# Two-layer MoE network on one core: expert choice by index among all 32 experts, counts issued later, two chunks gathered ahead, two-column Newton steps as tensor-scalar

## The chip, the cores and the metric

One NeuronCore of one Trainium2 chip runs the whole program in one launch. The metric is the device time of a run in microseconds (us); the kernel before takes 2264.09 us, the median of three runs.

## The reference

Two blocks of two layers follow each other on 256 tokens of width 1024, all in f32. The change lies in the first block, whose layers are an attention (layer 0) or a retention (layer 1) followed by a hierarchical mixture of experts. What that mixture computes:

```
p_group = softmax(xf @ wr_g + br_g);  pg, gi = top_k(p_group, 1)          # 4 groups
e_logits = (xf @ wr_e + br_e).reshape(T, 4, 8)
e_in = sum over groups of e_logits * one_hot(gi)                          # the 8 of the chosen group
pv, pi = top_k(softmax(e_in), 2)
gates = pg * pv / sum(pv);  expert_id = gi * 8 + pi
y = sum over both experts of gates * ((silu(a) * b) @ w_down[e]),  a, b = split(xf @ w_gu[e])
```

An expert's `w_gu` is 1024 x 1024 and its `w_down` 512 x 1024; there are 32 experts in each layer. The second block (gated recurrence, convolution, feed-forward) takes the first one's output; its context half does not depend on it and is woven into the mixtures as side work.

## The kernel before, in words

The program is written for Tile: each engine's instructions keep an order that a scheduler makes of the program's order and of priorities (`high_priority`), with semaphores for every dependence. All large weight loads are issued by SP on one queue, in order, each into one of a ring of 1 MB buffers (`wt`, `wload`, `wload2`); a load is issued when the last reader of its buffer is done.

A mixture (`moe`, from line 881) holds all 32 experts as 8 passes of 4 experts, each with 32 slots. It goes like this.

1. Ahead of it lie loads for the first steps: pairs k = 0 and 1 of pass 0, and four half tiles for k = 2 (lines 887 to 904), then further pairs into the ring as far as it reaches.
2. The router: `route_half` finishes the logits on TensorE (lines 857 and 861), `logits` (line 868) makes the root mean square of two token columns by `rsqrt` (line 223), and `choose` (line 762) finds group and experts on VectorE. There `top` is MAX8 and FIND_INDEX8 over the 4 group logits (padded to 8); line 781 masks the 32 expert logits by the group, line 782 sums them to 8; `top` again, over 8; lines 786 and 788 set a mask of 8 and `spread` (line 796) widens it to the 32-wide mask `M`.
3. Ranks: matmuls of `M` with triangles (lines 914 to 916), `rk` (line 919), and the one-hot places `oh` (line 926) of the first four experts, at high priority; those of the other 28 experts are called later, at k = 4, at normal priority.
4. The gather for pass 0: TensorE multiplies tokens by places, in eight chunks of 128 features (line 941), each copied out of PSUM into `xg` by ScalarE or VectorE in turn (lines 176 and 178). Three chunks are issued, then the counts of every expert (two matmuls, lines 952 and 953, and three VectorE instructions, lines 955 to 958), and then the gate/up products of pass 0.
5. Those run over k = 0 to 7 (line 999): 8 matmuls each, which the trace shows as 16, four experts side by side on column tiles of 32. For pass 0 each k from 1 on first issues the next chunk, so that at step k chunk k + 2 stands ahead of it, until there are no more. At k = 4 come the other places, the gates (`gates_of`), the overflow gates and the scatter matrix of pass 0.
6. Then silu, a product, four transposes and the down products (line 1019). Passes 1 to 7 follow, with the gather of each in the middle of the pass before. The counts are read as register values only in pass 7 (`overflow`), to see whether any expert has more than 32 tokens.

`rsqrt` starts from a bit trick and makes three Newton steps. One column takes two tensor-scalar instructions for a step (lines 241 and 242), more columns take three tensor-tensor instructions (lines 244 to 246). Two columns occur in `logits`, in `raw` (start of attention and of retention, line 364) and in `centred` (line 1229, in the second block's mixers).

Of the kernel before, what the change touches and what calls it, by code (L numbers as in the profile page):

```python
# [8 lines left out]
F32 = mybir.dt.float32  # L9
# [10 lines left out]
NEG = -1e30  # L20
# [10 lines left out]

C_ID, C_LE, C_LT, C_GE, C_ONE = 0, 128, 256, 384, 512
C_Z, C_LOW, C_UP = 640, 768, 896
C_IOTA, C_GRP, C_I8 = 1024, 1056, 1088
C_SEL, C_OFF = 1096, 1112
C_COS, C_SIN, C_RET = 1116, 1372, 1628
NCST = C_RET + 4 * 384


# [4 lines left out]
def constants():  # L44

    c = np.zeros((P, NCST), np.float64)
    r, q = np.arange(P)[:, None], np.arange(P)[None, :]
    c[:, C_ID:C_ID + P] = r == q
    c[:, C_LE:C_LE + P] = r <= q
    c[:, C_LT:C_LT + P] = r < q  # L50
    c[:, C_GE:C_GE + P] = r >= q
    c[:, C_ONE:C_ONE + P] = 1.0
    low, up = np.where(q <= r, 0.0, NEG), np.where(q >= r, 0.0, NEG)
    c[:, C_LOW:C_LOW + P] = low
    c[:, C_UP:C_UP + P] = up
    c[:, C_IOTA:C_IOTA + 32] = np.arange(1, 33)
    c[:, C_GRP:C_GRP + 32] = np.arange(32) // 8
    c[:, C_I8:C_I8 + 8] = np.arange(8)
# [34 lines left out]
class Net:  # L93
# [129 lines left out]
    def rsqrt(self, h, scaled=False):  # L223

        v, shape, n = self.nc.vector, list(h.shape), h.free_size()
        t = lambda k, d=F32: self.sm.tile(shape, d, tag="rs%s%d" % (k, n), name="rs")
        y, q = t("y", I32), t("q")
        v.tensor_scalar(y, h.bitcast(I32), -0.5, float(0x5f3759df), op0=ALU.mult, op1=ALU.add)
        y = y.bitcast(F32)
        if not scaled:  # L230
            g = t("g")
            v.tensor_scalar(g, h, -0.5, None, op0=ALU.mult)
        c = 1.0
        for _ in range(3):
            if scaled:
                v.tensor_scalar(q, y, h, y, op0=ALU.mult, op1=ALU.mult)
                v.tensor_scalar(y, q, -3.0 * c * c, y, op0=ALU.add, op1=ALU.mult)
                c = -2.0 * c ** 3
                continue
            if n == 1:  # L240
                v.tensor_scalar(q, y, g, y, op0=ALU.mult, op1=ALU.mult)
                v.tensor_scalar(y, q, 1.5, y, op0=ALU.add, op1=ALU.mult)
                continue
            v.tensor_tensor(q, y, y, op=ALU.mult)
            v.tensor_tensor(q, q, g, op=ALU.mult)
            v.scalar_tensor_tensor(y, q, 1.5, y, op0=ALU.add, op1=ALU.mult)
        assert not scaled or c == RS
        return y
# [513 lines left out]
    def choose(self, mp, L):  # L762


        nc, v = self.nc, self.nc.vector
        t = lambda n, *s, d=F32: mp.tile([P, 2] + list(s), d, name=n)
        grp = self.cst[:, C_GRP:C_GRP + 32]
        i8 = self.cst[:, C_I8:C_I8 + 8]

        def top(src, n):  # L770
            val, idx, f = t(n + "v", 8), t(n + "i", 8, d=U32), t(n + "f", 8)
            for b in range(2):
                v.max(out=val[:, b, :], in_=src[:, b, :])
            for b in range(2):
                v.max_index(out=idx[:, b, :], in_max=val[:, b, :], in_values=src[:, b, :])
            v.tensor_copy(f, idx)
            return val, f
        gv, gi = top(L[:, :, 0:8], "tg")
        sel, ein = t("sel", 32), t("ein", 8)
        for b in range(2):  # L780
            v.scalar_tensor_tensor(sel[:, b, :], grp, gi[:, b, 0:1], L[:, b, 8:40], op0=ALU.is_equal, op1=ALU.mult)
        v.tensor_reduce(ein, sel.rearrange("p b (g i) -> p b i g", g=4), axis=AX.X, op=ALU.add)
        ev, ei = top(ein, "te")
        m8, M = t("m8", 8), t("M", 32)
        for b in range(2):
            v.tensor_scalar(m8[:, b, :], i8, ei[:, b, 0:1], None, op0=ALU.is_equal)
        for b in range(2):
            v.scalar_tensor_tensor(m8[:, b, :], i8, ei[:, b, 1:2], m8[:, b, :], op0=ALU.is_equal, op1=ALU.add)
        self.spread(M, gi, m8)
        return M, gv, gi, ev, ei  # L790

    def spread(self, out, gi, w8):

        grp = self.cst[:, C_GRP:C_GRP + 32].rearrange("p (g i) -> p g i", g=4)
        for b in range(2):
            self.nc.vector.scalar_tensor_tensor(out[:, b, :].rearrange("p (g i) -> p g i", g=4), grp, gi[:, b, 0:1],
                                                w8[:, b:b + 1, :].to_broadcast([P, 4, 8]), op0=ALU.is_equal, op1=ALU.mult)

    def gates_of(self, mp, gv, gi, ev, ei):

        nc, v = self.nc, self.nc.vector
        t = lambda n, *s: mp.tile([P, 2] + list(s), F32, name=n)

        def softmax(val, n, name):
            neg, s = t(name + "n"), t(name + "s")
            p = t(name + "p", n)
            v.tensor_scalar(neg, val[:, :, 0], -1.0, None, op0=ALU.mult)
            for b in range(2):
                nc.scalar.activation(p[:, b, :], val[:, b, 0:n], AF.Exp, bias=neg[:, b:b + 1], accum_out=s[:, b:b + 1])
            v.reciprocal(s, s)  # L810
            v.tensor_tensor(p, p, s.rearrange("p (b o) -> p b o", o=1).to_broadcast([P, 2, n]), op=ALU.mult)
            return p
        pg, pe = softmax(gv, 4, "pg"), softmax(ev, 8, "pe")
        r, g2 = t("gr"), t("g2", 2)
        v.tensor_tensor(r, pe[:, :, 0], pe[:, :, 1], op=ALU.add)
        v.reciprocal(r, r)
        v.tensor_tensor(r, r, pg[:, :, 0], op=ALU.mult)
        v.tensor_tensor(g2, pe[:, :, 0:2], r.rearrange("p (b o) -> p b o", o=1).to_broadcast([P, 2, 2]), op=ALU.mult)
        a, c, G = t("ga", 8), t("gb", 8), t("G", 32)
        i8 = self.cst[:, C_I8:C_I8 + 8]  # L820
        for k, o in ((0, a), (1, c)):
            for b in range(2):
                v.tensor_scalar(o[:, b, :], i8, ei[:, b, k:k + 1], g2[:, b, k:k + 1], op0=ALU.is_equal, op1=ALU.mult)
        v.tensor_tensor(a, a, c, op=ALU.add)
        self.spread(G, gi, a)
        return G

    def route(self, l):
# [52 lines left out]
    def moe(self, l):  # L881
        nc, I, x, v = self.nc, self.I, self.x, self.nc.vector
        w_gu, w_down = I["expert_w_gu"][l], I["expert_w_down"][l]
        with ExitStack() as es:
# [61 lines left out]
                return xg, go()  # L946
            places(0, 4)
            xg, steps = gather(0, 1)
            for _ in range(3):
                next(steps, None)  # L950
            ps = self.g()
            nc.tensor.matmul(ps[:, 0:32], self.ones, M[:, 0, :], start=True, stop=False)
            nc.tensor.matmul(ps[:, 0:32], self.ones, M[:, 1, :], start=False, stop=True)
            cnt = mp.tile([P, 33], F32, name="cnt")
            v.tensor_copy(cnt[:, 0:32], ps[:, 0:32])
            v.tensor_reduce(cnt[:, 32:33], cnt[:, 0:32], axis=AX.X, op=ALU.max)
            cnti = mp.tile([P, 33], I32, name="cnti")
            v.tensor_copy(cnti, cnt)
            def placed(q):

                e0 = 4 * q
# [12 lines left out]
            for q in range(8):  # L974
# [975 lines left out]
```

## Time and profile before

| | |
|---|---|
| median of three runs (lowest, highest) | 2264.09 us (2264.05, 2270.21) |
| the profiled execution's own time | 2263.25 us |
| its span, first to last instruction | 2261.5 us |
| TensorE busy (matmuls) | 2093.2 us, 93% |
| VectorE, ScalarE, GpSimd busy | 1040.2, 715.6, 147.7 us |
| moved by DMA, mean | 681.91 MB, 302 GB/s |
| main DMA queue, share of the 16 engines' span | 80.6% |

The span is cut in 40 slices of 56.5 us for the busy rows of the page. The two mixtures are the stretches in which the DMA row stands at 9: roughly 200 to 735 us and 970 to 1540 us. Idle time is put down to the one who released the waiting engine last. A timeline row gives start, duration, engine, line, operation, output and inputs, and in brackets the idle time of the engine before it; several alike that follow closely are merged, with their count. A row of windows gives the busy time and the count of instructions on each engine, the granted TensorE clock as a share of full speed, the busy share of the DMA engines, and GB/s.

### The profile page before, as it was taken

To read this page: it belongs to the slowest core of one execution; us is meant where nothing else is said; L and a number is where in the kernel's file an instruction comes from. 1 tells how busy PE (TensorE), PEld (TensorE's weight loads), DVE (VectorE), ACT (ScalarE), POOL (GpSimd) and SP (SyncE) were. 2 spreads that over 40 slices of the span, in tenths; PEclk is the share of its full clock that TensorE was granted. 3 is DMA by queue.
4 is the path that set the end of the run, shared out by engine and by line. 5 is a ranking of instruction groups with operands and counts; after the bars stand their busy time and mean duration, and the time that the engine had idled before them with its cause. 6 is when DMAs were issued, how large, how long until landed. Compare 5 with 4: busy or idle time off the path is not lost. (4 is left out here: it accounts for less than half of the span.)

```text
span 2261.5 us, 32706 instructions
## 1 busy us (share of the span) xinstructions
PE 2093.2 (93%) x12772; PEld 1418.2 (63%) x12773; DVE 1040.2 (46%) x2555; ACT 715.6 (32%) x1492; POOL 147.7 (7%) x177
## 2 busy tenths in 40 slices
PE   8998889989987999989998999997999999999998
PEld 7766345535421876855563554353888998888997
DVE  6555224332110766640212212415687556687555
ACT  5353111121100434430000000113565555566554
POOL 1000000000000111000000000002211001211000
PEclk9999999999998999999999999998999999999999
DMA  8865999999999876779999999998755555555551
GB/s 265 322 237 207 412 410 409 376 410 406 369 414 394 322 278 232 262 285 404 406 405 407 406 405 402 407 392 292 247 169 178 186 186 169 191 167 192 187 187 65
DMA packets 283351, 681.91 MB, mean 302 GB/s; under 512 B 21840, under 2 KB 124664, under 8 KB 276920
## 3 DMA queue, kind: packets, MB, share of 16 engines
q1 hardware_dynamic: 283128, 679.73, 80.6%
q8 instruction: 102, 1.67, 0.3%
q14 instruction: 57, 0.47, 0.1%
q10 hardware_dynamic: 64, 0.03, 0.0%
HBM read 677.59 MB, written 2.10 MB: 301 GB/s over the span
## 5 line engine op out<-in xcount | busy, mean ns | idle before, releaser
L193 DVE TENSOR_TENSOR wl<-w,wh 128x512 fp32r<-128x512 f32 x568 | 392.0, 705 | 244.3 <-ACT wh L188 224.8
L188 ACT CAST wh<-w 128x512 fp32r<-128x512 f32 x600 | 363.9, 621 | 363.3 <-PE psm L446 108.8
L999 PE MATMUL psm<-w,xg 128*32 128x512 f32 x2016 | 293.0, 617 | 34.4 <-DMA w<-in_expert_w_gu_dram 31.1
L462 PE MATMUL psg<-xt,w 128*128 128x256 f32 x960 | 214.1, 381 | 7.1 <-DMA w<-in_w_in_dram 4.2
L462 PEld LDWEIGHTS psg<-xt,w 128*128 128x128 f32 x960 | 180.1, 190 | 47.9 <-issue 15.2
L999 PEld LDWEIGHTS psm<-w,xg 128*32 128x32 f32 x2016 | 64.5, 110 | 220.2 <-issue 143.4
L446 PE MATMUL psm<-xh,wh 128*128 128x256 f32 x640 | 178.9, 280 | 0.6 <-ACT ffh L1523 0.6
L446 PE MATMUL psm<-xh,wl 128*128 128x256 f32 x640 | 178.7, 279 | 0.0
L446 PE MATMUL psm<-xl,wh 128*128 128x256 f32 x640 | 178.6, 279 | 0.0
L446 PE MATMUL psg<-xh,wh 128*128 128x256 f32 x608 | 174.7, 287 | 3.6 <-ACT wh L188 2.2
L446 PE MATMUL psg<-xh,wl 128*128 128x256 f32 x608 | 172.6, 284 | 3.6 <-DVE wl L193 3.6
L1019 PE MATMUL psm<-w,hT 128*32 128x512 f32 (+1 forms) x1088 | 159.8, 596 | 16.4 <-DMA w<-in_expert_w_down_dram 13.6
L446 PE MATMUL psg<-xl,wh 128*128 128x256 f32 x608 | 171.0, 281 | 0.0
L1008 ACT ACTIVATE ha<-psm 128x512 f32<-128x512 f32 x16 | 9.6, 597 | 377.4 <-PE psm L999 337.8
L446 PEld LDWEIGHTS psg<-xh,wh 128*128 128x128 f32 x608 | 115.7, 190 | 19.4 <-ACT wh L188 8.4
L446 PEld LDWEIGHTS psm<-xh,wh 128*128 128x128 f32 x640 | 120.3, 188 | 1.9 <-ACT ffh L1523 1.1
L446 PEld LDWEIGHTS psm<-xh,wl 128*128 128x128 f32 x640 | 120.3, 188 | 0.8
L446 PEld LDWEIGHTS psm<-xl,wh 128*128 128x128 f32 x640 | 120.3, 188 | 0.0
L446 PEld LDWEIGHTS psg<-xh,wl 128*128 128x128 f32 x608 | 115.7, 190 | 6.7 <-DVE wl L193 6.3
L446 PEld LDWEIGHTS psg<-xl,wh 128*128 128x128 f32 x608 | 115.7, 190 | 0.0
L385 DVE TENSOR_TENSOR psg<-psg,g 128x512 f32<-128x512 f32 x64 | 44.7, 698 | 113.7 <-PE psg L1569 70.5
L1019 PEld LDWEIGHTS psm<-w,hT 128*32 128x32 f32 x1088 | 36.2, 112 | 94.1 <-issue 58.8
(507 smaller groups left out, 3285.9 us busy)
## 6 DMA issues: line engine op xcount, KB each, us to landing
w<-in_expert_w_gu_dram SPq DMA_DIRECT2D x252, 1024.0 KB
w<-in_expert_w_down_dram SPq DMA_DIRECT2D x120, 1024.0 KB
w<-in_w_gu_dram SPq DMA_DIRECT2D x66, 1024.0 KB
w<-in_w_mod_dram SPq DMA_DIRECT2D x48, 1024.0 KB
w<-in_w_in_dram SPq DMA_DIRECT2D x40, 1024.0 KB
w<-in_w_down_dram SPq DMA_DIRECT2D x33, 1024.0 KB
w<-in_ret_w_in_dram SPq DMA_DIRECT2D x24, 1024.0 KB
w<-in_fox_w_in_dram SPq DMA_DIRECT2D x16, 1024.0 KB
```

Of the source, the lines that this page charges most:

```text
L188: nc.scalar.copy(h, src)
L193: eng.tensor_tensor(l, src, h.bitcast(F32), op=ALU.subtract)
L385: self.nc.vector.tensor_tensor(o, o, g, op=ALU.mult)
L446: self.nc.tensor.matmul(o, a, x, start=i == 0, stop=i == len(mm) - 1)
L462: self.nc.tensor.matmul(o, w[:, k, c * P:(c + 1) * P], x[:, k0 + k, :], start=k0 == 0 and k == 0 and c % 2 == 0, stop=k0 == 4 and k == 3 a ...
L999: nc.tensor.matmul(gu[32 * j:32 * j + 32, half * 512:(half + 1) * 512], xg[:, k, 32 * j:32 * j + 32], ws[j][:, half * 512:(half + 1) * 512 ...
L1008: nc.scalar.activation(ha, gu[:, 0:512], AF.Silu)
L1019: nc.tensor.matmul(o[32 * j:32 * j + 32, :], hT[:, k, 32 * j:32 * j + 32], w(j), start=k == 0, stop=k == 3)
```

## The change

- `choose`: instead of masking and summing to 8 logits, VectorE adds -1e30 to the logits of the other groups (two tensor-scalar instructions of 32 columns and one tensor-tensor of 64) and takes the best of all 32. The indices then count among all 32 experts, so that `M` is made directly, by two tensor-scalar and two scalar-tensor-tensor instructions of 32 columns. `spread` is gone, here and in `gates_of`, where four tensor-scalar instructions now have 32 columns and one sum 64.
- The constants have 0 to 31 in place of 0 to 7; the offsets behind them move by 24 columns.
- Two chunks instead of three are gathered ahead of the gate/up products of pass 0, so that step k has chunk k + 1 ahead of it.
- The counts become a function that is called in pass 0 at k = 6.
- `rsqrt` with two columns makes each Newton step of four tensor-scalar instructions, one column each.

```diff
@@ rsqrt
             if n == 1:
                 v.tensor_scalar(q, y, g, y, op0=ALU.mult, op1=ALU.mult)
                 v.tensor_scalar(y, q, 1.5, y, op0=ALU.add, op1=ALU.mult)
                 continue
+            if n == 2:
+                for j in range(2):
+                    c = slice(j, j + 1)
+                    v.tensor_scalar(q[:, c], y[:, c], g[:, c], y[:, c], op0=ALU.mult, op1=ALU.mult)
+                for j in range(2):
+                    c = slice(j, j + 1)
+                    v.tensor_scalar(y[:, c], q[:, c], 1.5, y[:, c], op0=ALU.add, op1=ALU.mult)
+                continue
             v.tensor_tensor(q, y, y, op=ALU.mult)
@@ choose
         gv, gi = top(L[:, :, 0:8], "tg")
-        sel, ein = t("sel", 32), t("ein", 8)
+
+        ein = t("ein", 32)
         for b in range(2):
-            v.scalar_tensor_tensor(sel[:, b, :], grp, gi[:, b, 0:1], L[:, b, 8:40], op0=ALU.is_equal, op1=ALU.mult)
-        v.tensor_reduce(ein, sel.rearrange("p b (g i) -> p b i g", g=4), axis=AX.X, op=ALU.add)
+            v.tensor_scalar(ein[:, b, :], grp, gi[:, b, 0:1], NEG, op0=ALU.not_equal, op1=ALU.mult)
+        v.tensor_tensor(ein, ein, L[:, :, 8:40], op=ALU.add)
         ev, ei = top(ein, "te")
-        m8, M = t("m8", 8), t("M", 32)
+        M = t("M", 32)
         for b in range(2):
-            v.tensor_scalar(m8[:, b, :], i8, ei[:, b, 0:1], None, op0=ALU.is_equal)
+            v.tensor_scalar(M[:, b, :], i32, ei[:, b, 0:1], None, op0=ALU.is_equal)
         for b in range(2):
-            v.scalar_tensor_tensor(m8[:, b, :], i8, ei[:, b, 1:2], m8[:, b, :], op0=ALU.is_equal, op1=ALU.add)
-        self.spread(M, gi, m8)
-        return M, gv, gi, ev, ei
...
+            v.scalar_tensor_tensor(M[:, b, :], i32, ei[:, b, 1:2], M[:, b, :], op0=ALU.is_equal, op1=ALU.add)
+        return M, gv, ev, ei
@@ gates_of
-        a, c, G = t("ga", 8), t("gb", 8), t("G", 32)
-        i8 = self.cst[:, C_I8:C_I8 + 8]
-        for k, o in ((0, a), (1, c)):
+        c, G = t("gb", 32), t("G", 32)
+        i32 = self.cst[:, C_I32:C_I32 + 32]
+        for k, o in ((0, G), (1, c)):
             for b in range(2):
-                v.tensor_scalar(o[:, b, :], i8, ei[:, b, k:k + 1], g2[:, b, k:k + 1], op0=ALU.is_equal, op1=ALU.mult)
-        v.tensor_tensor(a, a, c, op=ALU.add)
-        self.spread(G, gi, a)
+                v.tensor_scalar(o[:, b, :], i32, ei[:, b, k:k + 1], g2[:, b, k:k + 1], op0=ALU.is_equal, op1=ALU.mult)
+        v.tensor_tensor(G, G, c, op=ALU.add)
         return G
@@ moe
             xg, steps = gather(0, 1)
-            for _ in range(3):
+            for _ in range(2):
                 next(steps, None)
-            ps = self.g()
-            nc.tensor.matmul(ps[:, 0:32], self.ones, M[:, 0, :], start=True, stop=False)
-            nc.tensor.matmul(ps[:, 0:32], self.ones, M[:, 1, :], start=False, stop=True)
-            cnt = mp.tile([P, 33], F32, name="cnt")
-            v.tensor_copy(cnt[:, 0:32], ps[:, 0:32])
-            v.tensor_reduce(cnt[:, 32:33], cnt[:, 0:32], axis=AX.X, op=ALU.max)
-            cnti = mp.tile([P, 33], I32, name="cnti")
-            v.tensor_copy(cnti, cnt)
+
+            def counts():
...
+                return cnti
+
@@ moe, pass q, step k
+                    if q == 0 and k == 6:
+                        cnti = counts()
                     ws = first.pop(0) if first else pair(q, k)
```

The body of `counts` is the seven removed lines.

## Rows read from the trace of the kernel before

**Rows 1.** The page: DMA share in 40 slices, and the gate/up matmuls' group.
```profile
DMA  8865999999999876779999999998755555555551
L999 PE MATMUL psm<-w,xg 128*32 128x512 f32 x2016 | 293.0, 617 | 34.4 <-DMA w<-in_expert_w_gu_dram 31.1
```

**Rows 2.** Windows of 2 us: layer 0, and one of layer 1.
```profile
core 0: us, PE busy (x) PEld busy (x) DVE busy (x) ACT busy (x) POOL busy (x), PEclk, DMA share, GB/s
210.00:212.00 2.00, 2.00 (x17) 1.66 (x20) 1.28 (x10) 0.37 (x1) 0.00 (x0) 0.69 0.70 250
...
220.00:222.00 2.00, 2.00 (x22) 0.85 (x14) 0.21 (x1) 0.37 (x1) 0.16 (x1) 1.00 0.26 81
...
982.00:984.00 2.00, 2.00 (x15) 0.55 (x8) 1.86 (x9) 0.00 (x0) 0.31 (x1) 0.83 0.00 0
```

**Rows 3.** Timeline of SP's load issues, layer 0, then layer 1.
```profile
215.96 0.38 SPq L156 DMA_DIRECT2D w<-in_expert_w_gu_dram  x1
...
220.92 0.90 SPq L156 DMA_DIRECT2D w<-in_expert_w_gu_dram  x2
...
993.91 3.38 SPq L156 DMA_DIRECT2D w<-in_expert_w_down_dram  x4
```

**Rows 4.** Timeline of TensorE behind the router, layer 0.
```profile
208.10 2.90 PE L941 MATMUL psg<-oh,xn 128*128 128x128 f32 x12 [0.73 <-DVE oh L926]
...
211.48 1.92 PE L999 MATMUL psm<-w,xg 128*32 128x512 f32 x16
```

**Rows 5.** Timeline of TensorE behind the router, layer 1.
```profile
977.38 2.90 PE L941 MATMUL psg<-oh,xn 128*128 128x128 f32 x12 [0.73 <-DVE oh L926]
980.07 0.47 PE L952 MATMUL psg<-M,cst 128*128 128x32 f32 x2
...
980.90 2.78 PE L999 MATMUL psm<-w,xg 128*32 128x512 f32 x16
983.61 0.71 PE L941 MATMUL psg<-oh,xn 128*128 128x128 f32 x4
984.25 1.92 PE L999 MATMUL psm<-w,xg 128*32 128x512 f32 x16
```

**Rows 6.** Timeline of VectorE in the router, layer 0.
```profile
199.79 0.16 DVE L244 TENSOR_TENSOR rs<-rs 128x2 f32<-128x2 f32 x1
199.99 0.16 DVE L245 TENSOR_TENSOR rs<-rs 128x2 f32<-128x2 f32 x1
...
200.72 0.24 DVE L876 TENSOR_TENSOR rp<-rp,psg 128x80 f32<-128x80 f32 x1 [0.57 <-PE psg L861]
...
202.24 0.43 DVE L878 SCALAR_TENSOR_TENSOR L<-rp,rs,br 128x40 f32<-128x40 f32 x2
...
203.40 0.41 DVE L781 SCALAR_TENSOR_TENSOR sel<-cst,tgf,L 128x32 f32<-128x32 f32 x2
203.85 0.27 DVE L782 TENSOR_REDUCE ein<-sel 128x16 f32<-128x64 f32 x1
204.15 0.24 DVE L773 MAX8 tev<-ein 128x8 f32<-128x8 f32 x2
...
205.24 0.36 DVE L788 SCALAR_TENSOR_TENSOR m<-cst,tef,m 128x8 f32<-128x8 f32 x2
205.52 0.41 DVE L796 SCALAR_TENSOR_TENSOR M<-cst,tgf,m 128x32 f32<-128x32 f32 x2
```

**Rows 7.** Timeline of the first two chunk copies, layer 0.
```profile
209.33 0.37 ACT L176 ACTIVATE xg<-psg,cols 128x128 f32<-128x128 f32 x1 [2.30 <-PE psg L941]
210.18 0.35 DVE L178 TENSOR_SCALAR xg<-psg,cols 128x128 f32<-128x128 f32 x1
```

**Rows 8.** Newton steps: groups by line, then two one-column chains interleaved.
```profile
L244 DVE TENSOR_TENSOR rs<-rs x39: 145/160/170, 9.8 to 2025.7; 128x2 f32<-128x2 f32 x30, 128x8 f32<-128x8 f32 x9
...
2254.71 0.46 DVE L241 TENSOR_SCALAR rs<-rs 128x1 f32<-128x1 f32 x2
2255.08 0.33 DVE L242 TENSOR_SCALAR rs<-rs 128x1 f32<-128x1 f32 x2
```

More of the change, by code (lines that the diff above doesn't have):

```diff
@@ L33 @@
 C_Z, C_LOW, C_UP = 640, 768, 896
-C_IOTA, C_GRP, C_I8 = 1024, 1056, 1088
-C_SEL, C_OFF = 1096, 1112
-C_COS, C_SIN, C_RET = 1116, 1372, 1628
+C_IOTA, C_GRP, C_I32 = 1024, 1056, 1088
+C_SEL, C_OFF = 1120, 1136
+C_COS, C_SIN, C_RET = 1140, 1396, 1652
 NCST = C_RET + 4 * 384
@@ L57, in constants @@
     c[:, C_GRP:C_GRP + 32] = np.arange(32) // 8
-    c[:, C_I8:C_I8 + 8] = np.arange(8)
+    c[:, C_I32:C_I32 + 32] = np.arange(32)
     c[:, C_SEL:C_SEL + 16] = r % 32 == np.arange(16)[None, :]
@@ L778, in choose, with gates_of @@
         gv, gi = top(L[:, :, 0:8], "tg")
-        sel, ein = t("sel", 32), t("ein", 8)
+        ein = t("ein", 32)
         for b in range(2):
-            v.scalar_tensor_tensor(sel[:, b, :], grp, gi[:, b, 0:1], L[:, b, 8:40], op0=ALU.is_equal, op1=ALU.mult)
-        v.tensor_reduce(ein, sel.rearrange("p b (g i) -> p b i g", g=4), axis=AX.X, op=ALU.add)
+            v.tensor_scalar(ein[:, b, :], grp, gi[:, b, 0:1], NEG, op0=ALU.not_equal, op1=ALU.mult)
+        v.tensor_tensor(ein, ein, L[:, :, 8:40], op=ALU.add)
         ev, ei = top(ein, "te")
-        m8, M = t("m8", 8), t("M", 32)
+        M = t("M", 32)
         for b in range(2):
-            v.tensor_scalar(m8[:, b, :], i8, ei[:, b, 0:1], None, op0=ALU.is_equal)
+            v.tensor_scalar(M[:, b, :], i32, ei[:, b, 0:1], None, op0=ALU.is_equal)
         for b in range(2):
-            v.scalar_tensor_tensor(m8[:, b, :], i8, ei[:, b, 1:2], m8[:, b, :], op0=ALU.is_equal, op1=ALU.add)
-        self.spread(M, gi, m8)
-        return M, gv, gi, ev, ei
[L792 to L799, printed above, removed]
+            v.scalar_tensor_tensor(M[:, b, :], i32, ei[:, b, 1:2], M[:, b, :], op0=ALU.is_equal, op1=ALU.add)
+        return M, gv, ev, ei
+    def gates_of(self, mp, gv, ev, ei):
         nc, v = self.nc, self.nc.vector
@@ L818, in gates_of @@
         v.tensor_tensor(g2, pe[:, :, 0:2], r.rearrange("p (b o) -> p b o", o=1).to_broadcast([P, 2, 2]), op=ALU.mult)
-        a, c, G = t("ga", 8), t("gb", 8), t("G", 32)
-        i8 = self.cst[:, C_I8:C_I8 + 8]
-        for k, o in ((0, a), (1, c)):
+        c, G = t("gb", 32), t("G", 32)
+        i32 = self.cst[:, C_I32:C_I32 + 32]
+        for k, o in ((0, G), (1, c)):
             for b in range(2):
-                v.tensor_scalar(o[:, b, :], i8, ei[:, b, k:k + 1], g2[:, b, k:k + 1], op0=ALU.is_equal, op1=ALU.mult)
-        v.tensor_tensor(a, a, c, op=ALU.add)
-        self.spread(G, gi, a)
+                v.tensor_scalar(o[:, b, :], i32, ei[:, b, k:k + 1], g2[:, b, k:k + 1], op0=ALU.is_equal, op1=ALU.mult)
+        v.tensor_tensor(G, G, c, op=ALU.add)
         return G
@@ L948, in moe @@
             xg, steps = gather(0, 1)
-            for _ in range(3):
+            for _ in range(2):
                 next(steps, None)
-            ps = self.g()
-            nc.tensor.matmul(ps[:, 0:32], self.ones, M[:, 0, :], start=True, stop=False)
-            nc.tensor.matmul(ps[:, 0:32], self.ones, M[:, 1, :], start=False, stop=True)
-            cnt = mp.tile([P, 33], F32, name="cnt")
-            v.tensor_copy(cnt[:, 0:32], ps[:, 0:32])
-            v.tensor_reduce(cnt[:, 32:33], cnt[:, 0:32], axis=AX.X, op=ALU.max)
-            cnti = mp.tile([P, 33], I32, name="cnti")
-            v.tensor_copy(cnti, cnt)
+            def counts():
+                ps = self.g()
+                nc.tensor.matmul(ps[:, 0:32], self.ones, M[:, 0, :], start=True, stop=False)
+                nc.tensor.matmul(ps[:, 0:32], self.ones, M[:, 1, :], start=False, stop=True)
+                cnt = mp.tile([P, 33], F32, name="cnt")
+                v.tensor_copy(cnt[:, 0:32], ps[:, 0:32])
+                v.tensor_reduce(cnt[:, 32:33], cnt[:, 0:32], axis=AX.X, op=ALU.max)
+                cnti = mp.tile([P, 33], I32, name="cnti")
+                v.tensor_copy(cnti, cnt)
+                return cnti
             def placed(q):
```

## The prediction

> **What bounds the kernel now.** I read the page's slices first, then windows of 2 us around the two routers, then the timelines of SP, TensorE and VectorE there. In the slices the reader is to see that both mixtures are stretches of DMA at 9 almost throughout, and that the gate/up matmuls have waited 31.1 us for their own weights [rows 1]. So a mixture is bound by its loads, and what counts is when the loads stand still. They do so behind each router: the buffers are full, TensorE cannot release any until the experts are chosen, and the DMA share falls to 0.00 in layer 1 and to 0.26 in a second gap of layer 0 [rows 2]. In layer 0 the next load goes out at 215.96, at the end of step k = 1, two more at 220.92, at the end of k = 3; in layer 1 the last of these releases is at 993.91, behind k = 4, from where four loads are queued at once [rows 3]. Whatever brings those releases forward shortens a gap of the DMA queue, and the rest of the mixture follows it. Work that TensorE does between router and k = 4 is therefore on the path; the same work at k = 6 is not.
>
> **Gather and counts.** Removed ahead of k = 0: one chunk and the counts. Three chunks take 2.69 us in layer 1, so 0.90 each, and the counts 0.83 until the first gate/up matmul (980.07 less 977.38, and 980.90 less 980.07 [rows 5]). So k = 0 may start 1.73 us earlier in layer 1, at 979.17 or so; in layer 0 two chunks of 0.90 behind 208.10 give 209.90 in place of 211.48, 1.58 earlier [rows 4]. The first chunk's copy is out by 209.70 [rows 7], so it does not hold this.
>
> But all this lies at a granted clock of 0.5. The share of 0.69 in the window from 210, with full speed at its end, puts the rise at 211.24 (0.76 us of it at full speed); 0.83 in the window from 982 puts it at 982.68 in layer 1 [rows 2]. If the rise stays where it is, k = 0 now runs at the lower clock in the place of what was removed. Its price at full clock is 1.92 [rows 4, 5]. Layer 0: 1.34 us at half clock make 0.67 of that, the other 1.25 end at 212.49 against 213.40, which is 0.91 gained. Layer 1: 3.50 us at half clock make 1.75, the other 0.17 end at 982.85 against 980.90 + 2.78 = 983.68, which is 0.83 gained. Later steps keep this: at each k from 1 to 5 one chunk goes ahead of the matmuls, as before (0.64 at full clock, 984.25 less 983.61 [rows 5]), only a later one. The two layers together: 1.74 us. If the rise came earlier with the work, the gain would be the full head start, 1.58 + 1.73 = 3.31 us. I take 1.74, since no row shows the rise tied to a count of matmuls. The page "TensorE: Matmul & The Clock Gate" of the Trainium skill, in Part 1 of it, says the warm-up is a matter of time and not of a number of matmuls; by that rule the sum is the 1.74, and without it the 3.31.
>
> At k = 6 come chunk 7 and the counts. They end no later than before against the loads: those of that stretch are queued since 220.92 and 993.91 [rows 3], and the pass waits for its weights anyway [rows 1]. Were that cover gone, they would cost about what they cost now at full clock, 0.64 and under 0.83. The three VectorE instructions of the counts leave a busy stretch of VectorE (1.86 of 2 us in the window from 982 [rows 2]) for an idle one; nobody waits for them until pass 7. The chunks' copies have one step of lead instead of two: 1.92 us of matmuls and the next chunk's 0.64 against a copy of 0.35 to 0.37 [rows 7]. That is enough unless VectorE is late by 2 us. No DMA is added, and none is issued from another place, so SP's order stays.
>
> **Choosing.** The masked sum took 0.75 us, 203.40 to 204.15 [rows 6]. Two tensor-scalar instructions of 32 columns take the place of two of the same width (0.45), and a sum of 64 columns the place of a reduction of 64 (0.30); tensor-tensor with two columns follows its predecessor by 0.20, so the sum costs between 0.20 and 0.30. I take 0.25, a gain of 0.05. MAX8 and FIND_INDEX8 now read 32 columns, four instructions in a row: a pair of 8 columns takes 0.36 and of 32 columns 0.41 (lines 788 and 796 [rows 6]), so 0.025 for one, 0.10 lost; the bounds are nothing and, were they charged for each of eight values, 0.8 lost. The last stage goes, 205.24 to 205.52, a gain of 0.28, less 0.05 for the wider masks. Together 0.18 earlier in each layer. The gates lose two instructions and get wider ones; they are on VectorE behind the first chunks and nobody waits for them before the scatter at k = 4: nothing.
>
> **Newton steps.** Before, a step is three dependent instructions 0.20 apart (199.79 and 199.99 [rows 6]), 0.60. After, it is two pairs. The trace has just this pattern, where two one-column chains run interleaved: the second pair starts 0.37 behind the first and is done 0.33 later [rows 8]. So a step is 0.57 to 0.70; I take 0.65, 0.05 more, and 0.15 more for three steps. There are ten calls (30 instructions of two columns, three to a call [rows 8]); two are in the routers and two at the start of attention and retention, the others in side work and mixers off the path. In the router part of the first step lies under a wait of 0.57 for the logits' matmuls (at 200.72 [rows 6]); where the scheduler puts that addition now is open, which is worth from 0.57 gained to 0.2 lost. I take 0.15 lost in each router, which cancels the 0.18 of the choosing, and nothing elsewhere (bounds: 0.3 lost, nothing gained).
>
> A rule of the Trainium skill speaks against this part: "VectorE: DVE Perf Modes", in its section on the errata, says that operations on SBUF pay a fixed latency for each instruction, so that four small ones cost more than three. By it a step is 0.80 and a call 0.60 dearer. The interleaved rows have 0.70 at most [rows 8].
>
> **Sum.** 1.74 gained, choosing and Newton together nothing: 1.7 us off. The profiled execution took 2263.25 us, 0.84 under the median, with a span of 2261.5; so 2261.5 for it and **2262.4 us** against the median of 2264.09. 0.3%, about what a measurement of this kernel can tell from no change, is 6.8 us, and this is a quarter of it.
>
> **Rivals.**
> - *The clock rises with the earlier gate/up steps.* 3.3 us off, 2260.8. For it: the rises of the two layers lie 3.1 and 5.3 us behind the first chunk [rows 2, 4, 5], not at one distance, so they hang on something else than the start; against it, the same rows: nothing says that it moves to our side.
> - *Newton as four serial instructions.* Place: the path through both routers and both starts. If each of the four follows the other by 0.20, a call takes 2.4 for 1.8, four calls 2.4 us, and the time is 2264.8, slower than before. It decides from 0.43 a call on. For it: one instruction more in each step, and in the router nothing else runs on VectorE to fill the gaps. Against it: rows 8. It is also what the errata section of that page of the Trainium skill would make of it.
> - *The gain does not get through.* By the end of k = 7 TensorE has done the same chunks and counts as before, and its total is unchanged; where TensorE and not the queue sets the pace, nothing is left: 2264.1. For it: TensorE is full in all windows of that stretch [rows 2]. Against it: 31.1 us of waits for weights [rows 1].
> - *Another order.* The scheduler orders all that follows anew. One gap like that of layer 0, from the window at 210 to 215.96 [rows 2, 3], some 4.6 us, may come or go in either layer: 2253 to 2272.
>
> **Chances.** Forecast 0.68, clock 0.08, Newton 0.07, no gain 0.09, another order 0.08. Predicted 2262.4. The first four lie between 2259.7 (the clock's, with 0.57 gained in both routers) and 2264.8, and the runs of the kernel before reach 6.2 us above their lowest; with part of the fifth the range is 2257.5 to 2266.8. Faster by over 0.3% (below 2257.3): 0.06, from another order and a clock that helps; slower (above 2270.9): 0.05, from another order and late copies; within: 0.89.
>
> **What would show it.** Right: TensorE's first gate/up matmul some 1.6 us earlier behind its first chunk, with two chunks and no counts ahead; the counts behind k = 5; the first load behind the router 0.8 to 0.9 us earlier against the router's first chunk; Newton pairs 0.37 and about 0.28 apart; `M` 0.2 us sooner behind the logits. Wrong: a TensorE wait for a chunk's copy at k = 1 to 5; a Newton step over 0.70; a MAX8 pair of 32 columns much above the 0.24 of 8 [rows 6]; a load gap as long as before; or a mixture whose length differs by more than the two gaps.

## The result, and the profile after

The changed kernel takes 2276.53 us, the median of five runs (2272.28 to 2278.94); the kernel before, beside it on the same chip, 2264.05 (2261.26 to 2270.21). The ratio is 1.0057, with an interval of 1.0043 to 1.0071: about 12 us slower, where 1.7 us off was forecast. The profiled execution has a span of 2274.8 us.

The page of the changed kernel: the DMA row and its GB/s in 40 slices of 57 us, and the gate/up matmuls' group (the line is now 1006). They answer to [rows 1].
```profile
DMA  7865999999999976779999999997755555555551
GB/s 255 314 237 195 402 404 405 397 406 399 380 409 386 320 278 231 275 283 404 406 404 407 406 405 402 407 384 271 248 165 184 185 186 168 190 184 173 186 186 65
...
L1006 PE MATMUL psm<-w,xg 128*32 128x512 f32 x2016 | 288.5, 612 | 38.4 <-DMA w<-in_expert_w_gu_dram 34.5
```

The GB/s row of the page before, which no group above shows:
```profile
GB/s 265 322 237 207 412 410 409 376 410 406 369 414 394 322 278 232 262 285 404 406 405 407 406 405 402 407 392 292 247 169 178 186 186 169 191 167 192 187 187 65
```
Two things are to be seen. The queue is no less full, but slices 5 to 7, in layer 0's mixture, moved 412, 410 and 409 GB/s before and 402, 404 and 405 after: the same loads run 1 to 2% slower. And the wait of the gate/up matmuls for weights has grown from 31.1 to 34.5 us. In layer 1 (slices 19 to 26) the two rows are alike.

Now the routers, where the forecast looked. VectorE in layer 0's router, after:
```profile
206.35 0.17 DVE L228 TENSOR_SCALAR rs<-rh 128x2 int32<-128x2 int32 x1
...
206.63 0.45 DVE L247 TENSOR_SCALAR rs<-rs 128x1 f32<-128x1 f32 x2
207.00 0.33 DVE L250 TENSOR_SCALAR rs<-rs 128x1 f32<-128x1 f32 x2
207.25 0.45 DVE L247 TENSOR_SCALAR rs<-rs 128x1 f32<-128x1 f32 x2
...
208.48 0.23 DVE L876 TENSOR_TENSOR rp<-rp,psg 128x80 f32<-128x80 f32 x1
208.74 0.43 DVE L878 SCALAR_TENSOR_TENSOR L<-rp,rs,br 128x40 f32<-128x40 f32 x2
...
209.90 0.39 DVE L790 TENSOR_SCALAR ein<-cst,tgf 128x32 f32<-128x32 f32 x2
...
210.58 0.29 DVE L781 MAX8 tev<-ein 128x8 f32<-128x32 f32 x2
...
211.78 0.41 DVE L797 SCALAR_TENSOR_TENSOR M<-cst,tef,M 128x32 f32<-128x32 f32 x2
```
A Newton step is 0.62 us (206.63 to 207.25), and all three now lie ahead of line 876, which no longer waits for the logits' matmuls as it did in [rows 6]. From `L` (line 878) to the end of `M` it is 3.45 us; before it was 3.69, from 202.24 to 205.52 + 0.41 [rows 6].

TensorE behind both routers, after, which answers to [rows 4] and [rows 5]:
```profile
214.36 2.05 PE L941 MATMUL psg<-oh,xn 128*128 128x128 f32 x8 [0.73 <-DVE oh L926]
216.34 2.78 PE L1006 MATMUL psm<-w,xg 128*32 128x512 f32 x16
219.05 0.71 PE L941 MATMUL psg<-oh,xn 128*128 128x128 f32 x4
...
984.28 2.04 PE L941 MATMUL psg<-oh,xn 128*128 128x128 f32 x8 [0.74 <-DVE oh L926]
986.26 3.52 PE L1006 MATMUL psm<-w,xg 128*32 128x512 f32 x16
```
The windows of the clock's rise (the last three numbers are granted clock, DMA share, GB/s), which answer to [rows 2]:
```profile
216.00:218.00 2.00, 2.00 (x10) 0.51 (x13) 1.80 (x11) 0.00 (x0) 0.00 (x0) 0.50 0.99 361
218.00:220.00 2.00, 2.00 (x20) 0.84 (x16) 1.35 (x6) 0.20 (x1) 0.77 (x3) 0.97 0.18 54
...
988.00:990.00 2.00, 2.00 (x14) 0.46 (x7) 1.45 (x7) 0.00 (x0) 0.56 (x2) 0.62 0.00 0
```
And SP's issues there, which answer to [rows 3]:
```profile
221.68 0.38 SPq L156 DMA_DIRECT2D w<-in_expert_w_gu_dram  x1
...
226.63 0.90 SPq L156 DMA_DIRECT2D w<-in_expert_w_gu_dram  x2
...
1000.01 3.38 SPq L156 DMA_DIRECT2D w<-in_expert_w_down_dram  x4
```
The first gate/up matmul follows the first chunk after 1.98 us in layer 0 (before 3.38), the first load after 7.32 (before 7.86), and in layer 1 the four loads after 15.73 (before 16.53). So the routers did about what was forecast. The loss is elsewhere.

To find it, the start of each TensorE matmul of the one trace was compared with that of the same matmul in the other. The difference, in us, worked out from the two traces, each number the median over 15 us from the place named (single executions; how far two of them may drift apart is told with the experiments):

| us of the kernel before | 15 | 60 | 150 | 195 | 225 | 735 | 960 | 990 | 1485 | 1545 | 2010 | 2085 | 2250 |
|---|---|---|---|---|---|---|---|---|---|---|---|---|---|
| after less before | 2.1 | 2.7 | 6.7 | 6.8 | 6.0 | 7.3 | 7.4 | 7.2 | 6.2 | 11.0 | 10.4 | 13.3 | 13.3 |

Half of the loss is there by 150 us, before any router has run. More comes at the end of layer 1's mixture and, at 2010 to 2085 us, in the second block's first mixer. Both first and last are places of the two-column Newton steps.

VectorE at the start of attention, before:
```profile
9.76 0.16 DVE L244 TENSOR_TENSOR rs<-rs 128x2 f32<-128x2 f32 x1
9.84 0.48 DVE L355 SCALAR_TENSOR_TENSOR xl<-psg,mixg,xh 128x256 fp32r<-128x256 f32 x1
10.23 0.15 DVE L245 TENSOR_TENSOR rs<-rs 128x2 f32<-128x2 f32 x1
10.30 0.47 DVE L355 SCALAR_TENSOR_TENSOR xl<-psg,mixg,xh 128x256 fp32r<-128x256 f32 x1
...
13.08 0.68 DVE L193 TENSOR_TENSOR wl<-w,wh 128x512 fp32r<-128x512 f32 x1
```
and after:
```profile
9.77 0.45 DVE L247 TENSOR_SCALAR rs<-rs 128x1 f32<-128x1 f32 x2
10.14 0.33 DVE L250 TENSOR_SCALAR rs<-rs 128x1 f32<-128x1 f32 x2
...
11.61 0.47 DVE L374 TENSOR_SCALAR w<-cst,rs 128x128 f32<-128x128 f32 x2
12.00 0.16 DVE L375 COPY rc<-rs 128x2 f32<-128x2 f32 x1
12.07 2.83 DVE L363 SCALAR_TENSOR_TENSOR xl<-psg,mixg,xh 128x256 fp32r<-128x256 f32 x7
14.81 1.89 DVE L193 TENSOR_TENSOR wl<-w,wh 128x512 fp32r<-128x512 f32 x3
```
Before, the nine Newton instructions stand one by one between the splits of the tokens (`xl`): the next instruction starts 0.07 to 0.08 us behind each of them. After, the three steps stand in one block of 1.84 us (9.77 to 11.61), the scales behind them, and only then the splits. `wl` comes 1.73 us later, and with it TensorE's second matmul of the first product. Before, then after:
```profile
13.81 0.58 PE L446 MATMUL psg<-xh,wl 128*128 128x256 f32 x1 [0.75 <-DVE wl L193]
```
```profile
15.55 0.58 PE L454 MATMUL psg<-xh,wl 128*128 128x256 f32 x1
```

### The profile page after: what moved, and what is told of

Its sections match the earlier page's. It is cut to its first block, busy times and chain, and to the rows that moved or that the text cites. A ratio compares the mean times of both kernels' runs of the same rounds, so it can differ in the third digit from the quotient of the medians.

```text
span 2274.8 us, 32726 instructions
## 1 busy us (share of the span) xinstructions
PE 2091.3 (92%) x12772; PEld 1419.9 (62%) x12773; DVE 1050.0 (46%) x2577; ACT 716.0 (31%) x1492; POOL 148.4 (7%) x177
## 5 line engine op out<-in xcount | busy, mean ns | idle before, releaser
L1006 PE MATMUL psm<-w,xg 128*32 128x512 f32 x2016 | 288.5, 612 | 38.4 <-DMA w<-in_expert_w_gu_dram 34.5
L1026 PE MATMUL psm<-w,hT 128*32 128x512 f32 (+1 forms) x1088 | 159.4, 591 | 18.9 <-DMA w<-in_expert_w_down_dram 16.1
```

The source lines that it names most:

```text
L1006: nc.tensor.matmul(gu[32 * j:32 * j + 32, half * 512:(half + 1) * 512], xg[:, k, 32 * j:32 * j + 32], ws[j][:, half * 512:(half + 1) * 512 ...
L1026: nc.tensor.matmul(o[32 * j:32 * j + 32, :], hT[:, k, 32 * j:32 * j + 32], w(j), start=k == 0, stop=k == 3)
```

## Experiments

Offsets in this section are those of the table above, of each kernel's profiled execution against that of the kernel before. Ratios, with their intervals in brackets, are against runs of the kernel before beside it on the same chip; its medians there were 2261.95 to 2266.18 us.

A single offset of 1 to 2 us is no evidence. Four kernels below whose start is that of the kernel before (the wider tile by 96 bytes, the wider DRAM tensor, the pairs in the mixers, the two chunks) are 1.4 to 2.2 us behind at 60 us. Most of it arises between 16 and 20 us: TensorE's clock reaches its higher level, 2.4 GHz, at 19.2 to 20.5 us in their traces and at 16.7 in that of the kernel before. From 20 to 150 us they drift by less than 0.6 us more.

**The change without its Newton branch, and the Newton branch alone.** The first kernel is the changed one less these lines, the second the kernel before with them.
```diff
+            if n == 2:
+                for j in range(2):
...
+                continue
```


> The change without its Newton part: two-column steps are three tensor-tensor instructions again; indices, counts and two chunks ahead stay. Theory N (the two-column pairs leave no gaps on VectorE, so what stood between the steps goes behind them, at the start of attention and in the second block): 2261 to 2264 us, TensorE's second matmul near 14 us instead of 15.6, and the mixers around 2030 us without their 2.8 us. Rival R (the routing part moves buffers and reorders SP's loads): 2270 us or more, with the loss of 4.8 us in the last pass of layer 1 still there.

Measured: 1.0013 [1.0003, 1.0022], at 2264.96 us just above the range of theory N. Its offset is 0.3 at 150 us, 3.6 at 735 and 3.7 at the end.

> The kernel before with the Newton part alone. Theory N: as slow as the whole change without the routers' gain of some 2 us, so 2276 to 2280 us. Rival R: 2265 to 2270 us, the 1.7 us at the start and the 2.8 us of the second block alone.

Measured: 1.0060 [1.0046, 1.0075], as much as the whole change; 7.2 at 150 us, 4.9 at 2010, 11.2 at 2085. The Newton steps carry the loss, at the two places of the table. What is left without them is a smaller loss in layer 0's mixture.

**Newton pairs at one place only**, in the kernel before: the first edit is in `raw` (start of attention and of retention), the second, of another kernel, in `centred` (the mixers).
```diff
...
-            rs = self.rsqrt(ms)
+            rs = self.rsqrt(ms, pairs=True)
```
```diff
...
-        rs = self.rstd(mv[:, :, 1], 1)
+        rs = self.rstd(mv[:, :, 1], 1, pairs=True)
```


> The kernel before with two-column Newton steps in pairs only at the start of attention and of retention. Theory N (the order on VectorE at the start delays the first low weight parts, and the order of the whole attention follows): 1 to 2 us late by 20 us, 6 to 7 us late by 150 us, none added at 2030 us; 2266 to 2271 us. Rival (it is the length of the steps): under 0.5 us late by 20 us and no more behind it; 2262 to 2263 us.

Measured: 1.0036 [1.0023, 1.0048]; 7.5 at 150 us.

> The kernel before with two-column Newton steps in pairs only in the mixers (centred). Theory N: nothing before 470 us, some 6 us late between 2010 and 2080 us, where the norm of the heads comes behind it; 2266 to 2270 us. Rival: 2262 to 2263 us, under 0.3 us in each place.

Measured: 1.0024 [1.0015, 1.0033]; 4.0 at 2010 and 6.8 at 2085 us. The time is as expected, the place only in part: 2.8 us arise between 2010 and 2085 us where some 6 were expected, and half of the 4.0 before it is the clock's rise at the start. The two ratios sum to the 1.0060 of all ten calls, so nothing is left for the two in the routers.

In the first mixer VectorE shows the same pattern. Before:
```profile
2023.05 0.16 DVE L244 TENSOR_TENSOR rs<-rs 128x2 f32<-128x2 f32 x1
...
2023.35 0.17 DVE L244 TENSOR_TENSOR rs<-rs 128x8 f32<-128x8 f32 x1
...
2027.29 1.83 DVE L1812 TENSOR_TENSOR hs<-hs,rs 128x512 f32<-128x512 f32 x2
```
After the whole change:
```profile
2032.71 0.45 DVE L247 TENSOR_SCALAR rs<-rs 128x1 f32<-128x1 f32 x2
...
2035.20 3.52 DVE L193 TENSOR_TENSOR wl<-w,wh 128x512 fp32r<-128x512 f32 x3
...
2039.77 0.16 DVE L220 TENSOR_SCALAR rsh<-hss 128x8 f32<-128x8 f32 x1
...
2046.21 1.29 DVE L1819 TENSOR_TENSOR hs<-hs,rs 128x512 f32<-128x512 f32 x2
```
Before, the two-column chain and the eight-column chain of `hs` run interleaved. After, the pairs come first, weight splits next, and the eight-column chain only begins at 2039.77; `hs` is 18.9 us later where the offset before it was 10.4.

**The order alone.** Is it the form of the steps, or where the other work stands? This kernel keeps the tensor-tensor steps and only holds the first weight splits back behind them.
```diff
-            v.tensor_copy(rc, rs)
+            put = v.tensor_copy(rc, rs)
+        if not late:
+            self.hold = put
```


> The kernel before, its Newton steps untouched (three tensor-tensor instructions each); at the start of attention and retention the splits of the first weight buffer are held back until the copy of rsqrt's result is done, so that these splits stand behind the Newton steps on VectorE as they do in the changed kernel. Theory 'order' (what was lost at the start is lost because the scheduler packs the Newton steps and puts the splits of xl and wl behind them, not because of the steps' length): TensorE's second matmul about 1 us or more later (13.81 to 15 or later), the offset grows to 3 to 7 us by 150 us, and the time is 1.0015 to 1.0035 of before. Rival 'form' (the tensor-scalar pairs themselves cost it): no pair is in this kernel, so the offset stays within 1 us and the time within 0.9990 to 1.0010.

Measured: 1.0018 [1.0009, 1.0027], an offset of 2.9 at 120 us and 5.3 at the end. TensorE in this kernel:
```profile
12.47 0.58 PE L448 MATMUL psg<-xh,wh 128*128 128x256 f32 x1 [2.58 <-ACT wh L188]
13.96 1.19 PE L373 MATMUL psg<-w,cst 128*128 128x256 f32 x2 [0.91 <-PE psg L448]
14.59 0.78 PE L448 MATMUL psg<-xh,wl 128*128 128x256 f32 x1
```
The second matmul of the product is at 14.59, 0.78 late and not a full 1 us: the splits of the tokens stayed between the steps, only those of the weights moved. From there the order of the whole stage differs and 0.8 becomes 3 us (0.8 until 40 us, 1.6 at 60, 3.1 at 75), where the kernels with an untouched start stay as they are. So an order costs this without any pair in the kernel; that all of the pairs' 1.0036 is order was not shown.

**The other parts alone**, in the kernel before. First kernel: `choose`, `gates_of` and the constants, as in the change.
```diff
-C_IOTA, C_GRP, C_I8 = 1024, 1056, 1088
+C_IOTA, C_GRP, C_I32 = 1024, 1056, 1088
...
```
Second kernel: the two chunks, and the counts at k = 6.
```diff
-            for _ in range(3):
+            for _ in range(2):
...
+                    if q == 0 and k == 6:
+                        cnti = counts()
```


> The kernel before with the indices among 32 experts alone (choose, gates, constants). Theory N: 2263.5 to 2265 us, the routers 0.1 to 0.2 us shorter. Rival R: slower by 2 us or more, with another order of the loads in the last passes.

Measured: 1.0031 [1.0020, 1.0042]; the offset grows from 0.9 at 225 to 5.3 at 735 us, all of it in layer 0's mixture. That is the rival's time without its reason: SP issues its loads in another order only between 217 and 247 us, and not in the last passes.

> The kernel before with two chunks ahead and the counts at k = 6 alone. Theory N: 2261.5 to 2263 us, each router's first release 0.8 to 0.9 us earlier. Rival R: slower by 2 us or more, with SP reading the counts behind more loads of pass 7 than before.

Measured: 1.0006 [0.9998, 1.0015]; the offset falls from 2.7 to 2.2 us over layer 1's router and mixture, and the time shows no gain: the 1.74 us of the forecast would be 0.9992, outside the interval. The two parts (1.0031 and 1.0006) and the whole without Newton (1.0013) add up to no better than 0.0024. Nor does a single offset tell a microsecond or two: the kernel with the larger DRAM tensor, below, ends 2.9 us behind in its profile at an equal median.

**Where the constants lie.** In the change without its Newton steps SP issues all its loads in the order of the kernel before, yet in layer 0's mixture they are slower. What else the change does is make the constants' tile 96 bytes a partition wider, and so move every buffer that is allocated behind it. First kernel: the tile wider on the chip only. Second: the tensor in DRAM wider only.
```diff
-        cst = cp.tile([P, C_COS], F32, name="cst")
+        cst = cp.tile([P, C_COS + 24], F32, name="cst")
...
```
```diff
-NCST = C_RET + 4 * 384
+NCST = C_RET + 4 * 384 + 24
...
```


> The kernel before, with 24 unused columns at the end of the constants' tile on chip, so that every buffer behind it lies 96 bytes further, as the new indices make it; nothing else. Theory A (the place of the weight buffers sets the time of a DMA packet): 2266 to 2270 us, mean packet of 4096 bytes in layer 0's mixture 164 ns instead of 162.2, gained offset some 4 to 5 us by 735 us. Rival (the place does nothing; what index cost is the order or the DRAM tensor): within 1 us of before, packets of 162.2 ns.

Measured: 1.0017 [1.0008, 1.0027].

> The kernel before, with the constants' tensor in DRAM 24 columns wider at its end, which no one reads; the tiles on chip stay where they are. Theory A: within 1 us of before, packets of 162.2 ns. Rival (where the tensors lie in DRAM): 2266 to 2270 us, packets of 164 ns.

Measured: 1.0000 [0.9991, 1.0009]. Their GB/s rows, the first kernel's and the second's:
```profile
GB/s 258 320 244 199 406 404 404 398 407 399 369 409 391 315 276 235 275 278 404 406 405 407 406 405 403 407 389 284 247 164 185 188 189 167 193 162 195 187 186 65
```
```profile
GB/s 258 319 245 198 413 406 410 377 399 405 368 414 396 322 276 233 277 272 404 406 405 407 407 404 403 407 391 292 249 169 182 186 186 169 191 167 192 187 186 65
```
Slices 5 to 7 are the row of the changed kernel in the one, about that of the kernel before in the other. The place on the chip slows the loads, not the size in DRAM. Of the 1.0031 of the routing it is 1.0017; the rest has no experiment of its own, and the two intervals overlap.

**Which places are good.** The kernel before with 16 columns more, 64 bytes; with 48, 192 bytes; and the change, without its Newton branch and whole, with 8 columns more than its own, which is 128 bytes more than in the kernel before. The first of these edits:
```diff
-        cst = cp.tile([P, C_COS], F32, name="cst")
+        cst = cp.tile([P, C_COS + 16], F32, name="cst")
...
```


> The kernel before with the constants' tile 16 columns wider on the chip only: a shift of 64 bytes. Theory 'multiples of 64 bytes are good': packets of 162.2 ns, 410 GB/s in the slices of layer 0's mixture, 0.9990 to 1.0010 of before. Rival 'only the place as it was, or a multiple of 128 bytes, is good': packets of 164 ns, 404 to 406 GB/s and 1.0008 to 1.0027 as with 96 bytes.

Measured: 0.9927 [0.9913, 0.9940], 16 us faster than the kernel before. Neither theory had this: one edit of one number, after which every instruction does the work that it did, gains more than the change was thought to move at all.

> The change without its Newton branch, with the constants' tile on the chip 8 columns wider still, so that all buffers behind it lie 128 bytes further than in the kernel before instead of 96. Theory 'offset of the buffers' (96 bytes is a bad offset for the loads, 128 a good one): the 4096-byte packets of layer 0's mixture are back from 164.0 to about 162.2 ns, the slices of that mixture back at 410 to 413 GB/s, layer 0's mixture no longer loses 3 to 4 us, and the time is 0.9975 to 0.9995 of before, some 4 us under the same kernel without the padding (1.0013). Rival 'any shift of the buffers costs': packets of 164 ns, slices of 402 to 406 GB/s and 1.0005 to 1.0025 of before.

Measured: 1.0012 [1.0003, 1.0021]; the rival was right, the padding helped nothing.

> The whole change with the constants' tile 8 columns wider, a shift of 128 bytes. If the costs add up (Newton 1.0060 alone, the offset 1.0017 alone, the earlier routers some 2 us gained): packets of 162.2 ns in layer 0's mixture and 1.0030 to 1.0045 of before, some 4 us under the change (1.0057). If the 128 bytes do not help: 1.0050 to 1.0070 and packets of 164 ns.

Measured: 1.0045 [1.0031, 1.0059], with the loads as slow as in the change.

> The kernel before with the constants' tile 48 columns (192 bytes) wider on the chip only: the ring's buffers begin 128 beyond a multiple of 256. Theory 'only multiples of 256 bytes are good': loads at 163.5 ns for a packet of 4096 bytes, 402 to 407 GB/s in the slices of both mixtures, and 1.0005 to 1.0030 of before. Rival 'multiples of 128 bytes are enough': 159 ns, 414 to 418 GB/s and 0.991 to 0.995 of before, as with 64 bytes.

Measured: 1.0000 [0.9991, 1.0010], below what the theory expected, though the loads are slow in both mixtures. The rows of the kernels with 64 and with 192 bytes:
```profile
GB/s 261 321 248 190 418 415 417 382 407 413 364 419 406 320 275 234 280 269 417 415 413 417 419 418 417 419 401 279 262 147 179 188 188 152 199 181 175 192 185 66
```
```profile
GB/s 259 322 240 204 407 403 405 385 407 399 382 409 389 318 277 234 272 271 404 406 405 407 407 405 403 408 391 290 248 170 183 187 186 169 191 164 194 186 186 65
```
With 64 bytes both mixtures run at 413 to 419 GB/s wherever the queue is full, with 192 at 403 to 409. The places can be read from the compiled kernels, the durations of packets from the traces' DMA records (worked out over 440 to 600 us, and 1300 to 1480 us):

| kernel | ring's buffers begin at | beyond a multiple of 256 | layer 0's two further buffers | 4096-byte packet, layer 0 | layer 1 |
|---|---|---|---|---|---|
| before | 50368 + 8192 n | 192 | 0 | 162.4 ns | 163.8 ns |
| 96 bytes more | 50464 + 8192 n | 32 | 96 | 163.9 | 163.7 |
| 128 more, no Newton | 50496 + 8192 n | 64 | 128 | 163.9 | 163.8 |
| 192 more | 50560 + 8192 n | 128 | 192 | 163.9 | 163.8 |
| 64 more | 50432 + 8192 n | 0 | 64 | 160.8 | 160.7 |

Load by load there are two kinds: loads whose packets take 159.0 ns and loads at 163.5. Which buffer a load fills is known from the compiled kernel, and its packets from the order of the queue. Counted as fast with a median packet of at most 160 ns, the loads of 1 MB behind the router are these:

| kernel, layer | into a place on a multiple of 256 | the first two behind such a load | all others |
|---|---|---|---|
| before, layer 0 | 41 of 41 fast | 35 of 46 | 10 of 82 |
| before, layer 1 | none there | none there | 11 of 181 |
| the change, layer 0 | none there | none there | 20 of 170 |
| 64 bytes more, layer 0 | 128 of 128 | 40 of 41 | none there |
| 64 bytes more, layer 1 | 180 of 180 | none there | none there |

Before, layer 0 has two buffers on a multiple of 256 bytes in a ring of eight, layer 1 none; with 64 bytes more, six of eight and eight of eight stand there. So a load into a place on a multiple of 256 bytes is fast, and so, mostly, are the next two loads, wherever they go: before, about half of layer 0's loads are fast, where two of eight buffers stand well. The change took the place from these two, and both kinds of fast loads went. This is also why the two further buffers of layer 0, off by 64 with 64 bytes more, cost nothing: they are always loaded right behind well-placed ones. Why the good place reaches on to the next loads stays open. All good places in these runs are odd multiples of 256; an even one was not tried.

The Trainium skill has a rule on such places, in "DMA: Bandwidth & Descriptors", section "How a descriptor splits into AXI transactions": a descriptor is cut at 256-byte boundaries, and one that starts off them pays for bytes that it does not use. The page tells it of the bytes read; here the place written is off. The traces agree on which place is good. By an estimate from the page's count of 32-byte beats, an offset of 192 would cost 6 beats more than the 128 of a 4096-byte packet, and one of 32 only 1; the traces have 163.5 ns for 32, 64, 128 and 192 alike, away from well-placed loads, so the price here does not grow with the offset.

**The change at the good place.** The slots' numbers (1 to 32) and the experts' (0 to 31) share one table of 33 columns, and the constants end 64 bytes further than before.
```diff
-C_IOTA, C_GRP, C_I32 = 1024, 1056, 1088
-C_SEL, C_OFF = 1120, 1136
-C_COS, C_SIN, C_RET = 1140, 1396, 1652
+C_IOTA, C_GRP, C_I32 = 1025, 1057, 1024
+C_SEL, C_OFF = 1112, 1128
+C_COS, C_SIN, C_RET = 1132, 1388, 1644
...
```


> The whole change with the constants repacked to 64 bytes more than before, not 96. If place and Newton steps add up: 1.0057 less 0.0017 for the bad place, less 0.0073 for the good one, so 0.995 to 0.998 of before, still 3 to 5 us slower than the same kernel without the Newton branch.

Measured: 0.9942 [0.9928, 0.9956], 2254.1 us, faster than expected or at the edge of it. Yet it is 10 us slower than the next kernel, the same without the Newton branch, where 3 to 5 were expected.

> The change without its Newton branch, its constants repacked (the slots' 1 to 32 and the experts' 0 to 31 share one table) to 64 bytes more than in the kernel before. Theory 'place and parts add up': 159 ns for a packet, 414 to 418 GB/s in both mixtures; the place alone gave 0.9927, this kernel at the bad place 1.0012 to 1.0013 where the bad place alone costs 1.0017; so 0.9915 to 0.9935. Rival 'with faster loads the routers' gain gets through twice': under 0.9910.

Measured: 0.9903 [0.9888, 0.9918], 2243.73 us beside 2266.18 for the kernel before: the fastest of all, and faster than the kernel before and the change by over 20 us. The middle is on the rival's side, the interval reaches into both: that the routers' gain gets through at the good place is not shown.

> As the whole change at 64 bytes, with the tensor-scalar Newton steps in the routers alone. Start and mixers were 1.0036 and 1.0024 by themselves, all ten calls 1.0060, so the routers' two calls are worth nothing either way: 0.9915 to 0.9935, within 0.001 of the change without the Newton branch at the same place. Rival 'the pairs cost in the router too': 0.994 to 0.996.

Measured: 0.9913 [0.9900, 0.9927], 2244.64 us. The pairs in the routers alone cost nothing that can be told; with them at start and mixers too the kernel is 10 us slower. The groups of the gate/up matmuls (their line is 997 in the fastest kernel, 999 in the kernel with 64 bytes more alone), in that order:
```profile
L997 PE MATMUL psm<-w,xg 128*32 128x512 f32 x2016 | 281.9, 607 | 28.9 <-DMA w<-in_expert_w_gu_dram 25.0
```
```profile
L999 PE MATMUL psm<-w,xg 128*32 128x512 f32 x2016 | 281.4, 608 | 28.4 <-DMA w<-in_expert_w_gu_dram 24.9
```
Waits for weights fell from 31.1 us [rows 1] to 25, and the matmuls' own busy time from 293.0 to 282; why the latter fell too was not tried.

## Why the prediction was wrong

*What held.* The first reading, that a mixture is bound by its loads, held: what gained most in this study was a shorter mean packet, 160.8 for 162.4 ns in layer 0 and 160.7 for 163.8 in layer 1. Inside the routers the steps came about as forecast. Choosing: forecast 0.18 us earlier, measured 0.24 (3.69 to 3.45). Newton in a router: forecast 0.15 lost by a step of 0.65; a step is 0.62, and since the wait for the logits now lies over the steps, the two together gained 0.50 (line 228 to the end of `M`: 6.34, from 199.59, to 5.84). Gather and counts: forecast 0.91 and 0.83 for the release of the loads against the first chunk, measured 0.54 and 0.80. The clock's rise did not come earlier with the work, as chosen: 3.1 us behind the first chunk before and 3.8 after in layer 0 (0.97 in the window from 218), 5.3 and 5.2 in layer 1 (0.62 in the window from 988). By an estimate from this, 0.6 us more at 1.2 in place of 2.4 GHz cost layer 0 some 0.3 us, most of what it is short. But the time shows nothing of the 1.74 us: the two chunks and the later counts by themselves are at 1.0006 [0.9998, 1.0015]. So far the rival that the gain does not get through was nearer than the forecast.

*The step that failed first* is the sentence on the Newton steps, "two are in the routers and two at the start of attention and retention, the others in side work and mixers off the path", priced at "nothing elsewhere (bounds: 0.3 lost, nothing gained)". It took the price of a step from the router, where VectorE has nothing else to do and three dependent instructions last 0.60. At the start VectorE is full: there a dependent instruction between independent ones holds the engine for 0.07 to 0.08, and a step costs 0.22. A pair fills its own gap, and the step costs 0.61. So a call at the start cost VectorE 1.84 and not 0.65 us, and the scheduler put the block ahead of the splits on which TensorE waits. The start alone is worth 1.0036, the mixers, called off the path, 1.0024; all ten calls 1.0060, some 14 us. The rival that had the starts among its places, four serial instructions, put 2.4 us on starts and routers by the wrong mechanism: the steps are not longer (0.62), what they displaced is.

*The second* is a term that the sum lacks. The diff moves the constants by 24 columns, and the prediction has no sentence on it. It moves every buffer behind them by 96 bytes; the two buffers of layer 0 that began on a multiple of 256 bytes lost that, and layer 0's mean packet went from 162.4 to 164.0 ns. Its price is small and not well fixed: 1.0017 with 96 bytes alone, 1.0000 with 192, where the loads are as slow. What it hid is large: the ring stood badly before and after.

*The third*, "SP's order stays", did not hold either: the counts are read on SP behind three more loads in the last pass of layer 1, and the load that went out at 1489.77 goes at 1502.32.
```profile
1484.46 11.77 SPq L156 DMA_DIRECT2D w<-in_expert_w_gu_dram  x6
1502.32 0.38 SPq L140 DMA_DIRECT2D w<-in_w_in_dram  x1
```
The change without its Newton steps has the same order (1499.18) and loses no such time there, so the 4.8 us of the table between 1485 and 1545 are not explained by it; they stay open, as the drift of single profiles does.

*The range* had one term for a new order of the scheduler, one gap of 4.6 us in a mixture, with 8 in 100. The order did change, but in the stages that no step had looked at.

## What to carry to other kernels

A small dependent chain has two prices: its latency where the engine is idle, and only its issue where the engine is full; before replacing it, look at what stands between its instructions in the trace, and at who waits for that. A table that grows moves every buffer behind it: look at where large load buffers begin, and place them on a multiple of 256 bytes first, since that was worth more here (0.7%) than all the other edits together. And price the parts of a diff that compute nothing, such as offsets.

## What was not expected of the hardware

Loads of 1 MB into buffers on a multiple of 256 bytes ran at 159.0 ns for each 4096-byte packet, and so, mostly, did the next two loads behind them (35 of 46 in the kernel before); the others ran at 163.5, whatever the offset. The kernel with most of its ring on such places was 16 us of 2262 faster. An early delay was not absorbed but grew: 0.78 us at the second matmul of attention became 2.9 us a hundred microseconds on (the kernel with the splits held back), and 1.7 became 6.7 in the change. That is more than the 0.3 to 2.2 us at 120 us of the kernels with an untouched start.
